# A bank freed inside the second operands of FFN 1, weights split at other places, a product order changed by one swap

## The chip, the cores and the metric

The program runs on one core of a Trainium2 chip. A core has a matrix engine (TensorE, PE in the profile), a vector engine (VectorE, DVE), a scalar engine (ScalarE, ACT), a general engine (GpSimd, POOL) and a queue engine (SyncE, SP) that issues most of the transfers. Each engine takes its instructions in the order of the program; semaphores tie the engines together. The metric is the device time of the program in microseconds, the median of three runs.

## The reference

A two-layer decoder trunk of width 1024 on 1024 tokens, in float32. Layer 0 mixes the tokens with a short gated convolution, layer 1 with dilated attention (16 heads of 64, three branches of window and dilation, a bias by distance); behind each mixer stands a SwiGLU network whose hidden width is 2816.

```
D_FF = ((8 * D_MODEL // 3 + 255) // 256) * 256
BRANCHES = ((128, 1), (512, 4), (2048, 16))

def short_conv_mixer(h, w_in, conv_k, w_out):
    b, c, u = jnp.split(h @ w_in, 3, axis=-1)
    y = lax.conv_general_dilated(
        c * u, conv_k[:, None, :].astype(u.dtype),
        window_strides=(1,), padding=[(CONV_WIDTH - 1, 0)],
        dimension_numbers=("NWC", "WIO", "NWC"),
        feature_group_count=D_MODEL)
    return (b * y) @ w_out

def dilated_attention_mixer(h, w_qkv, w_out, rel_bias):
    ...
    alpha = jax.nn.softmax(jnp.stack(lses, axis=0), axis=0)
    o = jnp.sum(alpha[..., None] * jnp.stack(outs, axis=0), axis=0)
    return o.reshape(bsz, seq, D_MODEL).astype(h.dtype) @ w_out

def swiglu(h, w_gate, w_up, w_down):
    return (jax.nn.silu(h @ w_gate) * (h @ w_up)) @ w_down

    for i in range(DEPTH):
        h = rms_norm(x, mix_norm[i])
        j = i // N_MIXERS
        if i % N_MIXERS == 0:
            x = x + short_conv_mixer(h, conv_w_in[j], conv_kernel[j], conv_w_out[j])
        else:
            x = x + dilated_attention_mixer(h, attn_w_qkv[j], attn_w_out[j], rel_bias)
        h = rms_norm(x, ffn_norm[i])
        x = x + swiglu(h, ffn_w_gate[i], ffn_w_up[i], ffn_w_down[i])
    return rms_norm(x, final_norm)
```

## The kernel before

**Precision.** A float32 product is made of three matmuls. `split` (L139, L140) cuts a tile into a high part, which ACT copies in the type fp32r, and a low part, which DVE gets by subtracting the high part. High times high, high times low and low times high are summed in a PSUM bank (L575, L576, L577). A weight comes from memory as `raw` (L151, issued by SP), some weights are first combined on DVE (`combo`, L191), and then they are split to `w`. `ensure(i)` makes the program split all weights up to number i of one list; `self.at(u, m)` gives the number of the weight of one product.

**Products.** The projections of the convolution (three of them) and of the gate and up parts of a SwiGLU use a scheme with seven products in place of eight (Winograd's form of Strassen's). A unit u is a block of output columns, and m from 1 to 7 is the product. A product (u, m) is 12 matmuls of 128x512: four blocks along the inner dimension, three matmuls each. `unit_order` (L258 to L285) is a list of the pairs, written by hand, and TensorE follows it.

**Banks.** There are eight PSUM banks. A unit has a bank p (products 1, 6, 7, 4, each added to what is in it) and a bank r (products 5 and 3). The first four units of a stage have product 2 in a bank q of its own. After products 1, 6 and 7, ACT copies p to a tile (`save`, L581: tiles u1, u2, u3), and the next product goes into p only behind that copy. `first(u)` adds q to u1 (L585, DVE); with it q is free. In FFN 1 the list begins with products 1 and 2 of units 0 to 3, which take all eight banks, and then has (4, 1).

**Operands.** The other factor of product m is a combination of the four quarters of the layer's input, in tiles `b` (high part by ACT at L567, low part by DVE at L568). `start(n)` is called ahead of the n-th product of the list and puts these preparations between the products, so that what it issues stands ahead of that product's saves in the queues of ACT and DVE. In a SwiGLU, `second_half` (from L1172) is a generator that makes the operands of products 7, 6, 4, 5 and 3 in steps: t3 is multiplied by rstd (L1181), the sums t2 and the differences f − t2, the multiplied h, and h − t2 follow. `mix` does this for the convolution (`start` at L1066 to L1125, with the operand sums at L936 and L937).

**Attention.** Heads are treated in pairs. Scores are at L1487 and L1488, the additions of the bias and the maxima behind them, the maximum over partitions on POOL (L1542), the exponentials at L1550 and L1551 (ACT), and the products with the values at L1561. `values` copies the two halves of its sums by ACT to z (the denominators, L1584) and o (L1585). `finish` takes the logarithm of z (L1616) and exp of its negative (L1618), multiplies o (L1610) and splits it to o_hi and o_lo; L369 to L371 multiply that with the output weights, and L506 adds to x. `first_weights` (L1632 to L1650) splits the first four weights of FFN 1 ahead, its high parts at L1644 and its low parts at L1648. The index `ahead_ao` says up to which output weight is split ahead of the last slot.

The function `after(n)` (L1817) is called behind each output block of FFN 0; it adds the block to the next norm's sums, and makes a step of the bias tables of attention.

Of the kernel before, what the change touches and what calls it, by code (L numbers as in the profile page):

```python
# [95 lines left out]
def trunk(ctx: ExitStack, tc: tile.TileContext, x, gains_in, cwi, ck, cwo, wqkv, wo, relb,  # L96
# [165 lines left out]
    def unit_order(nu, key):  # L262

        conv = key == CONV
        order = [(0, 1), (1, 1), (0, 2), (1, 2), (2, 1), (2, 2), (3, 1)]
        if conv:
            order += [(3, 2), (4, 1), (4, 2)] + [(u, m) for m in (6, 7, 5, 4, 3) for u in (0, 1)]
            order += [(2, 6), (2, 5), (2, 7)]
        else:
            if key:  # L270
                order = [(u, m) for m in (1, 2) for u in range(4)][:-1]
            order += [(3, 2)] + [(4, 1)] * key + [(u, m) for m in (6, 7, 4, 5, 3) for u in (0, 1)] + [(2, 6), (2, 5), (2, 7)]
        order += [(3, 6), (2, 4), (2, 3), (3, 5), (3, 7)] + [(4, 1)] * (key == 0) + [(3, 4), (3, 3)]
        if not conv:
            for u in range(4, SIMPLE):
                order += [(u, 6), (u, 5), (u, 7), (u + 1, 1), (u, 2), (u, 4), (u, 3)]
            for u in range(SIMPLE, nu, 2):
                order += [(u, 6), (u, 5), (u, 7), (u + 1, 1), (u, 3), (u + 1, 6), (u + 1, 5), (u + 1, 7)]
                deep = [(u + 1, DEEPER + i) for i in DEEP_ORDER]
                order += deep[:4] + [(u + 1, 3), deep[4]] + [(u + 2, 1)] * (u + 2 < nu) + deep[5:]  # L280
            return order
        for u in range(4, nu - 1):
            order += [(u, 6), (u, 5), (u, 7), (u + 1, 1), (u + 1, 2), (u, 4), (u, 3)]
        u = nu - 1
        return order + [(u, m) for m in (6, 5, 7, 4, 3)]  # L285

# [616 lines left out]
    class Conv(Strassen):  # L903
# [167 lines left out]
        def mix(self, group1):  # L1071
# [3 lines left out]
            def start(n):  # L1075
# [6 lines left out]
                elif n == 2:  # L1082
                    self.first(0)
                    ensure(self.at(4, 2))
                    next(prep)
                elif n == 3:
                    self.first(1)
                    combos[CONV, 0](6)
                elif n == 4:
# [16 lines left out]
                elif n == 10:  # L1106
                    ensure(self.at(1, 5))
                elif n == 11:
                    next(prep)
                elif n == 12:  # L1110
                    next(prep)
                    ensure(self.at(1, 4))
                elif n == 14:
                    next(prep, None)
                    ensure(self.at(1, 3))
                    X[:] = [None] * KT
                elif n == 18:
                    self.ahead = 3
# [21 lines left out]
    class Swiglu(Strassen):  # L1140
# [38 lines left out]
        def second_half(self):  # L1179
# [6 lines left out]
            for k in range(4):  # L1186
                tt(t3[k], t3[k], rstd, ALU.mult)
                low7.append(self.hi(7, k, t3[k]))
            for k in range(4):
                tt(t2[k], t3[k], f[k], ALU.add)  # L1190
# [42 lines left out]
        def feed_forward(self, stats, last_step, after, final=None):  # L1233
            prep = []

            def start(n):
# [130 lines left out]
    def attention(norm):  # L1367
# [107 lines left out]
        def scores(p, a, st):  # L1475
# [34 lines left out]
            m = page("m")  # L1510
            st["m"] = m
            yield

            for j in range(0, 8, 2):
                b = bank()
                for i in range(2):
# [4 lines left out]
                    else:  # L1521
# [32 lines left out]
        def values(p, a, st):  # L1554
            lf, lh, ld, lp = (st[n] for n in ("lf", "lh", "ld", "lp"))
            acc = [bank(), bank()]
            kd = [[128, 4], [1, 32]]
# [21 lines left out]
            o, z = st["o"], st["z"]  # L1579
            n0 = slice(64 * a, 64 * a + 64)  # L1580
            z0 = slice(64 - 64 * a, 128 - 64 * a)
            for ih in range(2):
                s = slice(ih * HALF, (ih + 1) * HALF)
                nc.scalar.activation(z[n0, s], acc[ih][z0], AF.Copy)  # L1584
                nc.scalar.activation(o[n0, s], acc[ih][n0], AF.Copy)  # L1585
            yield

        def finish(p):
# [25 lines left out]

            next(weights)
            nc.scalar.activation(z, z, AF.Ln)  # L1616
# [192 lines left out]
    with tc.tile_pool(name="first", bufs=1) as scope["pool"]:  # L1809
# [158 lines left out]
```

## Time and profile before

| | |
|---|---|
| time, median of three runs | 2168.83 us (2168.51 to 2171.3) |
| profiled execution | 2170.33 us, its span 2168.5 us |
| mean granted clock of TensorE | 0.994 |
| VectorE, adds at L585 | 153.8 us in 328 instructions |
| transfers | 306.72 MB, mean 141 GB/s |

The row of the engines' busy time, the list of waits and the timelines are in the prediction. A row of a timeline gives the start in us from the beginning of the span, the duration, engine, line, operation, what it writes and reads, the count, and in brackets the idle time of the engine ahead of it with what ended it. A wait is put down to the releaser that came last.

### The profile page before, as it was taken

The page shows a single profiled execution, that of the slowest core. Times are in us where ns is not written, and L with a number is a line of the kernel's source. Part 1 is how long each engine was busy: PE and PEld are TensorE (multiplying, and loading weights), DVE is VectorE, ACT ScalarE, POOL GpSimd, SP SyncE. Part 2 cuts the span into 40 slices and gives each one's busy share as a digit, 9 for nine tenths or more (in the row PEclk, how much of TensorE's full clock was granted, in tenths as well). Part 3 has the DMA queues.
Part 4 walks back from the last instruction along what each step waited for, and adds up shares of the span by engine and source line. Part 5 has one row for each costly group of instructions (what it writes and reads, how often), then busy time and mean ns, then how long its engine had stood idle before and what let it go on. Part 6 is the DMA issues. An engine that isn't in the chain of part 4 may idle for free.

```text
span 2168.5 us, 30735 instructions
## 1 busy us (share of the span) xinstructions
PE 2125.6 (98%) x11086; PEld 1818.7 (84%) x11086; DVE 1728.9 (80%) x3160; ACT 1002.3 (46%) x1797; POOL 222.7 (10%) x316
## 2 busy tenths in 40 slices
PE   9999999999999999999999999999799999999998
PEld 7788887888888888879999998887688888888887
DVE  7898769888888888864777676867788898888886
ACT  7433426444544444334545454536434444534435
POOL 2000001111212000010111111110011211100000
PEclk9999999999999999999999999999899999999999
DMA  7222643335545774341333233544024555586432
GB/s 210 68 93 68 228 141 88 126 122 168 168 156 185 270 284 160 91 149 47 91 83 104 81 105 106 167 135 151 25 93 141 165 173 173 170 315 225 160 93 78
DMA packets 148067, 306.72 MB, mean 141 GB/s; under 512 B 49850, under 2 KB 61130, under 8 KB 147914
## 3 DMA queue, kind: packets, MB, share of 16 engines
q1 hardware_dynamic: 82026, 206.83, 29.9%
q0 software_dynamic: 25872, 79.02, 10.4%
q10 hardware_dynamic: 40016, 18.90, 3.0%
q8 instruction: 88, 1.44, 0.3%
q14 instruction: 65, 0.53, 0.1%
HBM read 209.06 MB, written 88.28 MB: 137 GB/s over the span
## 4 chain that ended last, share of the span: by engine, by line
PE 75%; issue 11%; DVE 6%; DMA 4%; ACT 3%; POOL 1%; SPq 0%; POOLq 0%; ACTq 0%; DVEq 0%
PE bank L575 16%; PE bank L577 16%; PE bank L576 16%; PE bank L369 4%; PE bank L371 4%; PE bank L370 4%; PE bank L1561 4%; PE bank L670 2%; PE bank L673 2%; PE bank L672 2%; PE bank L1488 1%; PE bank L1487 1%; DMA acc<-sq 1%; PE bank L1428 1%; PE bank L1427 1%
## 5 line engine op out<-in xcount | busy, mean ns | idle before, releaser
L575 PE MATMUL bank<-b,w 128*128 128x512 f32 x1816 | 711.4, 392 | 18.9 <-DVE part L585 15.4
L577 PE MATMUL bank<-b,w 128*128 128x512 f32 x1816 | 708.2, 390 | 2.3 <-DVE w L140 2.3
L576 PE MATMUL bank<-b,w 128*128 128x512 f32 x1816 | 709.0, 390 | 0.5 <-DVE b L916 0.5
L575 PEld LDWEIGHTS bank<-b,w 128*128 128x128 f32 x1816 | 341.9, 188 | 93.5 <-DVE part L585 13.5
L577 PEld LDWEIGHTS bank<-b,w 128*128 128x128 f32 x1816 | 341.6, 188 | 74.7 <-DVE w L140 3.8
L576 PEld LDWEIGHTS bank<-b,w 128*128 128x128 f32 x1816 | 341.9, 188 | 71.5 <-DVE b L916 1.8
L139 ACT ACTIVATE w<-combo 128x512 fp32r<-128x512 f32 (+2 forms) x448 | 229.1, 540 | 244.5 <-DVE combo L191 224.4
L140 DVE TENSOR_TENSOR w<-combo,w 128x512 fp32r<-128x512 f32 (+2 forms) x448 | 254.0, 580 | 27.5 <-ACT w L139 27.2
L581 ACT ACTIVATE part<-bank 128x512 f32<-128x512 f32 x168 | 100.1, 596 | 309.4 <-PE bank L577 305.9
L140 DVE TENSOR_TENSOR w<-raw,w 128x512 fp32r<-128x512 f32 (+2 forms) x308 | 169.0, 567 | 26.6 <-ACT w L139 26.4
L585 DVE TENSOR_TENSOR part<-part,bank 128x256 f32<-128x256 f32 (+1 forms) x328 | 153.8, 498 | 38.5 <-ACT part L581 23.8
L139 ACT ACTIVATE w<-raw 128x512 fp32r<-128x512 f32 (+2 forms) x308 | 151.0, 527 | 68.6 <-DMA raw<-in_ffn_w_down 18.0
L831 DVE TENSOR_TENSOR x<-x,bank 128x512 f32<-128x512 f32 x168 | 114.4, 681 | 37.6 <-PE bank L577 33.8
L369 PE MATMUL bank<-w_hi,w 128*128 128x512 f32 (+1 forms) x320 | 120.1, 375 | 0.0
L371 PE MATMUL bank<-w_hi,w 128*128 128x512 f32 (+1 forms) x320 | 118.1, 369 | 0.9 <-DVE w L140 0.9
L370 PE MATMUL bank<-w_lo,w 128*128 128x512 f32 (+1 forms) x320 | 118.0, 369 | 0.0
L506 DVE TENSOR_TENSOR x<-x,bank 128x512 f32<-128x512 f32 (+1 forms) x104 | 65.8, 642 | 60.9 <-PE bank L371 52.2
L369 PE MATMUL bank<-h_hi,w_hi 128*128 128x512 f32 x256 | 104.5, 408 | 0.0
L191 DVE TENSOR_TENSOR combo<-raw 128x512 f32<-128x512 f32 (+1 forms) x160 | 102.9, 643 | 0.0
L371 PE MATMUL bank<-h_hi,w_lo 128*128 128x512 f32 x256 | 100.1, 391 | 0.2 <-DVE w_lo L140 0.2
L370 PE MATMUL bank<-h_lo,w_hi 128*128 128x512 f32 x256 | 100.0, 390 | 0.0
L1542 POOL PARTITION_ALL_REDUCE mb<-m x16 | 53.1, 3317 | 399.2 <-DVE m L1539 216.6
(265 smaller groups left out, 3808.7 us busy)
## 6 DMA issues: line engine op xcount, KB each, us to landing
hin<-part SPq DMA_DIRECT2D x126, 256.0 KB
raw<-in_ffn_w_gate SPq DMA_DIRECT2D x44, 512.0 KB
raw<-in_ffn_w_up SPq DMA_DIRECT2D x44, 512.0 KB
b<-ready SPq DMA_DIRECT2D x42, 512.0 KB
part<-sum POOLq DMA_DIRECT2D x72, 256.0 KB, 3.6
raw<-in_ffn_w_down SPq DMA_DIRECT2D x48, 384.0 KB
x<-spill SPq DMA_DIRECT2D x24, 512.0 KB
raw<-in_attn_w_qkv SPq DMA_DIRECT2D x24, 512.0 KB
```

Of the source, the lines that this page charges most:

```text
L139: nc.scalar.activation(hi, src, AF.Copy)
L140: eng.tensor_tensor(out=lo, in0=src, in1=hi, op=ALU.subtract)
L191: eng.tensor_tensor(out=c, in0=a, in1=b, op=op)
L369: nc.tensor.matmul(b, whi[:, a], ahi[:, s], start=first, stop=False)
L370: nc.tensor.matmul(b, whi[:, a], alo[:, s], start=False, stop=False)
L371: nc.tensor.matmul(b, wlo[:, a], ahi[:, s], start=False, stop=last)
L575: nc.tensor.matmul(b, hi[:, a], bhi, start=start and k == 0, stop=False, skip_group_check=True)
L576: nc.tensor.matmul(b, hi[:, a], blo, start=False, stop=False, skip_group_check=True)
L577: nc.tensor.matmul(b, lo[:, a], bhi, start=False, stop=k == n - 1, skip_group_check=True)
L581: nc.scalar.activation(t, b, AF.Copy)
L585: nc.vector.tensor_tensor(out=t, in0=t, in1=b, op=ALU.add)
L831: nc.vector.tensor_tensor(out=X[n][:, half(h)], in0=X[n][:, half(h)], in1=b, op=ALU.add)
```

## The change

It has five parts, and the arithmetic stays as it was.

- **Unit order.** In the list, (3, 7) stands ahead of (3, 5), and in the last unit of the convolution 7 stands ahead of 5.
- **Convolution start.** `ensure(self.at(4, 2))` goes behind `first(1)`, with `self.at(3, 2)` left where it was; weights (1, 4) and (0, 3) are split ahead of the operand steps of n = 12 and n = 14.
- **SwiGLU start.** In FFN 1, `second_half` stops behind t3, and its next step begins with `first(0)`, now taken at n = 4, with its own step; and at each operand step the weight of the product three places on is split ahead of it, in both networks.
- **Attention.** `values` copies a half of z and o as soon as its four blocks are done, in place of both at the end; the maxima of the second half stand ahead of the loop, those of the first at j = 2 in place of 4. At the end, three output weights in place of seven are split ahead of the last slot, the logarithm's table is loaded and the weights of FFN 1 are stepped there, and the other four slabs follow behind the slot.
- **`after(n)`** splits its weight ahead of `norm.add(n)`.

```diff
@@ unit_order
-        order += [(3, 6), (2, 4), (2, 3), (3, 5), (3, 7)] + [(4, 1)] * (key == 0) + [(3, 4), (3, 3)]
+        order += [(3, 6), (2, 4), (2, 3), (3, 7), (3, 5)] + [(4, 1)] * (key == 0) + [(3, 4), (3, 3)]
...
-        return order + [(u, m) for m in (6, 5, 7, 4, 3)]
+        return order + [(u, m) for m in (6, 7, 5, 4, 3)]
@@ mix, start
                 elif n == 2:
                     self.first(0)
-                    ensure(self.at(4, 2))
+                    ensure(self.at(3, 2))
                     next(prep)
                 elif n == 3:
                     self.first(1)
+                    ensure(self.at(4, 2))
                     combos[CONV, 0](6)
...
                 elif n == 12:
+                    ensure(self.at(1, 4))
                     next(prep)
-                    ensure(self.at(1, 4))
                 elif n == 14:
+                    ensure(self.at(0, 3))
                     next(prep, None)
                     ensure(self.at(1, 3))
@@ second_half
                 tt(t3[k], t3[k], rstd, ALU.mult)
                 low7.append(self.hi(7, k, t3[k]))
+            if self.key:
+                yield
+                self.first(0)
             for k in range(4):
                 tt(t2[k], t3[k], f[k], ALU.add)
@@ feed_forward, start
                 elif n == 4:
                     ensure(self.at(1, 7))
-                elif n in (5, 7, 8, 9, 11):
+                if n in (5, 7, 8, 9, 11) or n == 4 and self.key:
+                    ensure(self.base + n + 3)
                     next(prep[0], None)
@@ scores
             m = page("m")
             st["m"] = m
+            nc.vector.tensor_tensor(out=m[:, HALF:], in0=lf[:, HALF:], in1=lh, op=ALU.max)
             yield
...
-                if j == 0:
-                    nc.vector.tensor_tensor(out=m[:, HALF:], in0=lf[:, HALF:], in1=lh, op=ALU.max)
-                if j == 4:
+                if j == 2:
                     nc.vector.tensor_tensor(out=m[:, :HALF], in0=lf[:, :HALF], in1=ld[:, :HALF], op=ALU.max)
@@ values
                     mm(j // 4, off, b1, j - 1, view(lp, blk(j), b1), last=j % 4 == 3)
+                if j % 4 == 3:
+                    ih, s = j // 4, half(j // 4)
+                    nc.scalar.activation(z[n0, s], acc[ih][z0], AF.Copy)
+                    nc.scalar.activation(o[n0, s], acc[ih][n0], AF.Copy)
                 yield
...
-            for ih in range(2):
-                s = slice(ih * HALF, (ih + 1) * HALF)
-                nc.scalar.activation(z[n0, s], acc[ih][z0], AF.Copy)
-                nc.scalar.activation(o[n0, s], acc[ih][n0], AF.Copy)
-            yield
@@ finish
-            next(weights)
             nc.scalar.activation(z, z, AF.Ln)
@@ attention
-        ahead_ao = [k for k, f in ops].index(("ao", 1, AO_WIDE + 1))
+        ahead_ao = [k for k, f in ops].index(("ao", 1, 2))
...
         ensure(ahead_ao)
+        next(weights)
+        nc.scalar.activation(scratch, eps, AF.Ln)
         slot(H, dense, 20)
         run(dense)
+        ensure(ahead_ao + 4)
@@ after
+            if n in (0, 2):
+                ensure(op_state[1] + 1)
             norm.add(n)
             nc.gpsimd.dma_start(spill[n], X[n])
             if n in (0, 2):
-                ensure(op_state[1] + 1)
                 next(tab, None)
```

What this does to the queues is seen at three places. First VectorE at the start of FFN 1, before. The rows with `x<-x,rstd` are t3 and, further down, h; L568 makes low parts of operands, L140 those of weights, and L585 is the add of `first(0)`.

```order
L140 TENSOR_TENSOR w<-raw,w 128x512 x3
L140 TENSOR_TENSOR w<-combo,w 128x512 x2
L1181 TENSOR_TENSOR x<-x,rstd 128x512 x4
L1181 TENSOR_TENSOR x<-x,hcol 128x512 x2
...
L568 TENSOR_TENSOR b<-x,b 128x512 x6
L140 TENSOR_TENSOR w<-combo,w 128x512 x2
L1181 TENSOR_TENSOR hcol<-hcol,x 128x512 x4
L1181 TENSOR_TENSOR x<-x,rstd 128x512 x4
L568 TENSOR_TENSOR b<-hcol,b 128x512 x4
L1181 TENSOR_TENSOR hcol<-x 128x512 x4
L585 TENSOR_TENSOR part<-part,bank 128x512
```

The same place in the changed kernel, where the lines are two further on:

```order
L140 TENSOR_TENSOR w<-raw,w 128x512 x3
L140 TENSOR_TENSOR w<-combo,w 128x512 x2
L1183 TENSOR_TENSOR x<-x,rstd 128x512 x4
L140 TENSOR_TENSOR w<-combo,w 128x512 x2
L585 TENSOR_TENSOR part<-part,bank 128x512
L1183 TENSOR_TENSOR x<-x,hcol 128x512 x2
...
L568 TENSOR_TENSOR b<-x,b 128x512 x6
L1183 TENSOR_TENSOR hcol<-hcol,x 128x512 x4
L1183 TENSOR_TENSOR x<-x,rstd 128x512 x4
L568 TENSOR_TENSOR b<-hcol,b 128x512 x4
L1183 TENSOR_TENSOR hcol<-x 128x512 x4
```

The add and the pair of weights that stood behind the operands of products 7 and 6 now stand ahead of them. On ScalarE at the same place, in the changed kernel, L567 makes high parts of operands, L581 is a save, and the rows from `x` and `hcol` are the operands 7, 6, 4 and 5 in turn:

```order
L567 ACTIVATE b<-x 128x512 x4
L1258 ACT_TABLE_LOAD
L1258 ACTIVATE scratch<-eps 128x1
L139 ACTIVATE w<-combo 128x512 x2
L567 ACTIVATE b<-x 128x512 x4
L567 ACTIVATE b<-hcol 128x512 x4
L581 ACTIVATE part<-bank 128x512 x2
L567 ACTIVATE b<-hcol 128x512 x4
L581 ACTIVATE part<-bank 128x512
```

Before, the first row had eight copies and the fifth was missing; the saves stand behind the operands 4 and 5 in both. Last, ScalarE at the end of attention in the changed kernel: from the last weights (`raw`, three in place of seven) over the copies of z and o to the operand o_hi of the output product.

```order
L139 ACTIVATE w<-raw 128x384 x3
L1771 ACT_TABLE_LOAD
L1771 ACTIVATE scratch<-eps 128x1
L1588 ACTIVATE z<-bank 64x512
L1589 ACTIVATE o<-bank 64x512
...
L1619 ACTIVATE z<-z 128x1024
L1621 ACT_TABLE_LOAD
L1621 ACTIVATE z<-z 128x512
L139 ACTIVATE o_hi<-o 128x512
...
L139 ACTIVATE w<-raw 128x384 x4
```

Four weights went from ahead of the copies to behind the second o_hi, and a table load from behind the copies to ahead of them.

More of the change, by code (lines that the diff above doesn't have):

```diff
@@ L1555, in values @@
             lf, lh, ld, lp = (st[n] for n in ("lf", "lh", "ld", "lp"))
+            o, z = st["o"], st["z"]
+            n0 = slice(64 * a, 64 * a + 64)
+            z0 = slice(64 - 64 * a, 128 - 64 * a)
             acc = [bank(), bank()]
@@ L1577, in values @@
                     mm(j // 4, off, b1, j - 1, view(lp, blk(j), b1), last=j % 4 == 3)
+                if j % 4 == 3:
+                    ih, s = j // 4, half(j // 4)
+                    nc.scalar.activation(z[n0, s], acc[ih][z0], AF.Copy)
+                    nc.scalar.activation(o[n0, s], acc[ih][n0], AF.Copy)
                 yield
-            o, z = st["o"], st["z"]
-            n0 = slice(64 * a, 64 * a + 64)
-            z0 = slice(64 - 64 * a, 128 - 64 * a)
-            for ih in range(2):
-                s = slice(ih * HALF, (ih + 1) * HALF)
-                nc.scalar.activation(z[n0, s], acc[ih][z0], AF.Copy)
-                nc.scalar.activation(o[n0, s], acc[ih][n0], AF.Copy)
-            yield
         def finish(p):
```

## The prediction

> **What bounds the kernel now.** I read the page first, then the list of what TensorE waited for, then the timelines around the longest of those waits. In the page, the row of TensorE (PE):
>
> ```profile
> PE 2125.6 (98%) x11086; PEld 1818.7 (84%) x11086; DVE 1728.9 (80%) x3160; ACT 1002.3 (46%) x1797; POOL 222.7 (10%) x316
> ```
>
> TensorE bounds the whole span, and the change moves none of its instructions. So the time can change only by the gaps between matmuls. The waits of TensorE, by line, with their total, count and longest:
>
> ```profile
> PE bank L575 <- DVE part L585: 15.4, 2, 13.0
> PE bank L369 <- ACT o_hi L139: 3.3, 1, 3.3
> PE bank L1487 <- ACT o L1585: 2.3, 4, 0.6
> PE bank L577 <- DVE w L140: 2.3, 3, 1.0
> PE bank L1561 <- ACT lf L1551: 2.3, 3, 1.1
> PE bank L575 <- ACT part L581: 2.1, 3, 0.7
> PE bank L575 <- ACT w L139: 0.9, 2, 0.6
> ```
>
> Two rows hold most of it. Their matmuls, with the last product before the long wait, and the granted clock (in a window's row the third number from the end) around the two longest waits:
>
> ```profile
> 1527.36 0.39 PE L575 MATMUL bank<-b,w 128*128 128x512 f32 x1
> 1529.86 0.39 PE L577 MATMUL bank<-b,w 128*128 128x512 f32 x1
> 1543.29 0.79 PE L575 MATMUL bank<-b,w 128*128 128x512 f32 x1 [13.04 <-DVE part L585]
> 1548.57 0.63 PE L575 MATMUL bank<-b,w 128*128 128x512 f32 x1
> ...
> 1471.67 0.80 PE L369 MATMUL bank<-o_hi,w 128*128 128x512 f32 x1 [3.29 <-ACT o_hi L139]
> ...
> 34.62 0.47 PE L575 MATMUL bank<-b,w 128*128 128x512 f32 x1 [2.36 <-DVE part L585]
> ...
> 1470.62:1477.45 6.83, 5.78 (x13) 4.28 (x14) 5.27 (x10) 3.08 (x6) 0.00 (x0) 0.50 0.06 25
> 1535.47:1549.13 13.66, 5.84 (x14) 4.59 (x15) 7.76 (x13) 0.97 (x3) 0.00 (x0) 0.50 0.00 0
> ```
>
> The first two rows are the first and the last matmul of one product: 11 steps in 2.50 us, 0.227 us each, 2.72 us a product. From 1543.29 to 1548.57 twelve steps take 5.28 us: behind a long wait the clock is half (0.50), and the stretch of half speed costs 5.28 − 2.72 = 2.6 us and a little more at its edge, 2.8. After 3.29 us of waiting the 13 matmuls until 1477.45 took 5.78 us instead of 13 × 0.227 = 2.95: 2.8 again. After 2.36 us the next matmul took 0.47 and the pace was full again: no half speed.
>
> **FFN 1 start: bank and operands.** The vector engine (DVE) and ScalarE (ACT) there, before:
>
> ```profile
> 1521.89 2.49 DVE L1181 TENSOR_TENSOR x<-x,rstd 128x512 f32<-128x512 f32 x4
> 1531.72 1.28 DVE L140 TENSOR_TENSOR w<-combo,w 128x512 fp32r<-128x512 f32 x2
> 1532.92 2.49 DVE L1181 TENSOR_TENSOR hcol<-hcol,x 128x512 f32<-128x512 f32 x4
> 1535.33 2.49 DVE L1181 TENSOR_TENSOR x<-x,rstd 128x512 f32<-128x512 f32 x4
> 1537.74 2.49 DVE L568 TENSOR_TENSOR b<-hcol,b 128x512 fp32r<-128x512 f32 x4
> 1540.14 2.49 DVE L1181 TENSOR_TENSOR hcol<-x 128x512 f32<-128x512 f32 x4
> 1542.55 0.68 DVE L585 TENSOR_TENSOR part<-part,bank 128x512 f32<-128x512 f32 x1
> ...
> 1522.61 3.64 ACT L567 ACTIVATE b<-x 128x512 fp32r<-128x512 f32 x6 [2.45 <-DVE x L1181]
> 1528.87 1.28 ACT L1253 ACT_TABLE_LOAD   x1
> 1530.28 1.13 ACT L139 ACTIVATE w<-combo 128x512 fp32r<-128x512 f32 x2
> 1533.72 2.40 ACT L567 ACTIVATE b<-hcol 128x512 fp32r<-128x512 f32 x4 [2.31 <-DVE hcol L1181]
> 1548.81 0.60 ACT L581 ACTIVATE part<-bank 128x512 f32<-128x512 f32 x1 [12.69 <-PE bank L577]
> ```
>
> The add that frees the bank for product (4,1) stands last of some 30 operand instructions. In the new order it follows t3 and one pair of weights. ACT: the four copies of t3 end at 1522.61 + 4 × 0.60 = 1525.0, the table load at 1526.3, the pair of weights at 1527.5; DVE's L140 pair runs from 1527.1 to 1528.3, the add to 1529.0. The product before ends at 1530.08, so the wait of 13.04 us goes, with 1.1 us to spare.
>
> What is late next: DVE has 12 operand instructions of 0.60 behind the add (to 1536.3), then the four rows of 2.41 that stand at 1532.92 to 1540.14, now 3.4 us later. ACT takes its instructions in order. The saves of (4,1) and (0,6) stand behind the four L567 of operand 4, which end at 1539.4; two saves at 0.60 let product (0,7) start at 1540.6 where it could at 1538.24 (1530.08 + 3 × 2.72): **2.4 us**. The save of (1,6) stands behind operand 5, whose last input comes at 1546.1; copy and save bring 1547.3, where (1,7) could start at 1543.3: **4.0 us**. One product later (0,4) starts at 1550.1; now it does so at 1559.8 (1548.57, the slow edge of 0.3, and four products). That is 9.7 us less before any new half speed. A wait of 4.0 us is longer than the 3.29 that brought it, so I charge one stretch, 2.8: **6.9 us** (without it 9.7; with two stretches 4.1).
>
> [...]
>
> **Product order of unit 3 and of the last unit.** Product (3,7) comes ahead of (3,5), and in the last unit of the convolution 7 ahead of 5, so that a product stands between the save of product 5 and product 4 or 3 in its bank:
>
> ```profile
> 95.23 0.50 PE L575 MATMUL bank<-b,w 128*128 128x512 f32 x1 [0.69 <-ACT part L581]
> ```
>
> This is one of the three waits of the row with 2.1 us; with the slow restart (0.50 against 0.39, the next step 0.33) each is 0.85. A save takes 0.60, the product now between takes 2.72. **2.5 us**; nothing if a product's weights came late instead.
>
> **Attention's end.** ACT before, from the last weights to the operand that TensorE waited for:
>
> ```profile
> 1458.55 0.53 ACT L139 ACTIVATE w<-raw 128x384 fp32r<-128x384 f32 x1 [0.46 <-DVE w_lo L140]
> 1463.43 0.59 ACT L1584 ACTIVATE z<-bank 64x512 f32<-64x512 f32 x1
> 1465.87 1.28 ACT L1616 ACT_TABLE_LOAD   x1
> 1467.16 1.06 ACT L1616 ACTIVATE z<-z 128x1024 f32<-128x1024 f32 x1
> 1469.54 0.63 ACT L1618 ACTIVATE z<-z 128x512 f32<-128x512 f32 x1
> 1470.99 0.63 ACT L139 ACTIVATE o_hi<-o 128x512 fp32r<-128x512 f32 x1 [0.82 <-DVE o L1610]
> ```
>
> Four of seven weight slabs leave the queue ahead of 1463.43; the table of Ln is loaded ahead of the copies. The third slab ends at 1459.1, the load at 1460.4, four copies at 0.61 at 1462.9, Ln 1464.0, the load for Exp 1465.3, Exp 1465.9, product and o_hi 1467.4. TensorE's earlier work ends at 1468.2: the wait (3.45 with its restart) and the stretch of half speed (2.8) go. The four slabs now come behind o_hi: the first has its low half at about 1471.7, where the tenth matmul wants it at 1470.7. So 6.25 − 1.05 = **5.2 us**; 2.4 if half speed comes all the same, 6.25 if the slab is in time.
>
> [...]
>
> **Convolution start.** DVE before:
>
> ```profile
> 23.09 1.29 DVE L140 TENSOR_TENSOR w<-raw,w 128x512 fp32r<-128x512 f32 x2 [0.54 <-ACT w L139]
> 26.31 0.69 DVE L140 TENSOR_TENSOR w<-raw,w 128x512 fp32r<-128x512 f32 x1 [1.93 <-ACT w L139]
> 33.80 0.68 DVE L585 TENSOR_TENSOR part<-part,bank 128x512 f32<-128x512 f32 x1
> ```
>
> The weights of (4,1) and (4,2), which waited for a transfer until 26.31, now stand behind the add of 33.80. The seven operand instructions before that add took 4.95 us from 28.85; from 24.3 they bring it to 29.3. But the low weights of (4,1) come behind it, at 30.5, some 0.8 late. Of the 2.52 of this wait 1.75 go. Further on, weights (1,4) and (0,3) are split ahead of operands: four waits (0.9 in the L139 row, 1.77 of the 2.3 in the L140 row) go with their restarts, 3.3; the operand low halves come three DVE instructions later, 1.8 us, of which I charge 1.5. Together **3.5 us**; 0 if DVE's backlog eats it, 5 if the operands are covered.
>
> **Small edits.** Weights ahead of operands at FFN 0 take the third L140 wait, 0.56 and restart: **0.7**. Two waits of weights lose about two thirds, one L140 (0.60) coming earlier in each: **1.2**.
>
> ```profile
> 957.89 0.50 PE L371 MATMUL bank<-w_hi,w 128*128 128x512 f32 x1 [0.85 <-DVE w L140]
> 1444.71 0.50 PE L371 MATMUL bank<-w_hi,w_lo 128*128 128x512 f32 x1 [0.83 <-DVE w_lo L140]
> ```
>
> Attention's copies by half were in this order on ACT already, and the bank that L1487 waits for (0.6 each) is still one of those copied last: these waits stay. The maxima of the softmax come earlier, and with them POOL's reduction, so the three L1561 waits (2.3, 2.8 with restarts) shrink, between 0 and 2.8: I take the middle, **1.4**. SP's queue has the spill loads ahead of three weight loads at attention's end; those weights are split later than before, which covers it.
>
> **Sum.** 6.9 + 2.5 + 5.2 + 3.5 + 0.7 + 1.2 + 1.4 = 21.4 us. The profiled execution took 2170.33 (span 2168.5), which would be 2148.9; the median of the runs, 2168.83, is 1.5 lower, so the forecast is **2147.4**.
>
> **Rivals.** *The saves don't bind* (ACT runs ahead of DVE's operands, or half speed stays away): FFN 1 gains up to 16 (13.2 + 2.8), and with the upper ends of the others the time is about 2138. For it: FFN 0 has the same steps and no such wait. Against: there no table load and no add stand in the chain. Chance 0.13. *Half of it is given back* (new waits for weights at the convolution and attention's end, a second stretch at FFN 1): 4.1 (FFN 1) + 2.4 (attention's end) + 2.5 (order) + 1 (convolution) + 1 (the small ones) = 11, time 2158. For it: each of these places has a margin of 1 us or less. Chance 0.22. *The change doesn't do what it says*: the add stays behind the weights of (1,7) because ACT's table load is late. Then the bank comes a little late, 1 to 3 us, but not 13; it lies in the former. *Slower*: half speed that persists. At FFN 1 two waits follow each other within 8 us; if every window behind them stays at 0.50, each us of it costs half a us, and 21.4 us are lost after 43 us, 13 windows of 3.41. Against: at 1549.13 and 1477.45 the clock came back as soon as one window was full of matmuls. It decides only from 43 us on, then 2172 to 2176. Chance 0.02.
>
> **How the numbers follow.** Forecast 0.60, the first rival 0.13, the second 0.22, no gain at all (2165 to 2173) 0.03, slower 0.02. A measurement of this kernel tells about 0.2%, 4.3 us. Faster 0.95, same 0.03, slower 0.02. The range reaches from 2136 to 2158, and leaves out about 2 in 10.
>
> **What would show it.** Right: L575's wait for L585 falls from 15.4 below 2; in its place waits of L575 for L581 near 2.4 and 4.0 behind the start of FFN 1, with one stretch of half speed; no wait of L369 for o_hi, full clock there; no L581 waits of 0.7. Wrong: saves without a wait (more gain), or DVE's wait for w at the convolution growing (less).

## The result and the profile after

The changed kernel takes 2151.82 us in the median of four runs (2150.50 to 2153.65), the kernel before 2169.06 (2168.51 to 2171.30). The ratio is 0.9919 with a 95% interval of 0.9902 to 0.9936: faster by 17 us (0.8%), where 21.4 were forecast. The profiled execution has a span of 2151.1 us against 2168.5.

The engines' busy time on the page after the change:

```profile
PE 2122.8 (99%) x11086; PEld 1817.6 (84%) x11086; DVE 1728.4 (80%) x3160; ACT 1002.3 (47%) x1798; POOL 221.2 (10%) x316
```

And what TensorE waited for, by line (the lines have moved: L1487 is L1493 now, L1561 is L1569):

```profile
PE bank L575 <- ACT part L581: 6.5, 3, 3.6
PE bank L1493 <- ACT o L1589: 2.3, 4, 0.6
PE bank L575 <- DVE part L585: 1.6, 1, 1.6
PE bank L575 <- ACT w L139: 1.4, 2, 1.2
PE bank L576 <- DVE b L568: 1.2, 1, 1.2
PE bank L371 <- DVE w L140: 1.1, 1, 1.1
PE bank L369 <- ACT o_hi L139: 1.1, 1, 1.1
```

The wait of 13.0 us for the add at L585 is gone, and so are the three for lf. At the top now are waits for saves (L581), as the forecast had it; further down stand one for L585 that it had not, and one for o_hi (1.1 us) that it said would go.

Both programs issue the same 11086 matmuls in the same order but for the two swaps. So the start of the n-th matmul in one profile against its start in the other gives the lead that the changed kernel has at that point, and where it wins or loses. All times are in us from the start of the span; a slow window is a stretch of 3.41 us at half clock (0.50 from 942.91 to 946.32 in the changed kernel).

| matmul | before | after | lead | what lies ahead of it |
|---|---|---|---|---|
| 280 | 72.53 | 68.78 | 3.8 | the convolution's start |
| 400 | 100.80 | 96.06 | 4.7 | the swap in unit 3 |
| 1040 | 246.84 | 243.96 | 2.9 | the convolution's last unit |
| 1640 | 383.74 | 380.89 | 2.9 | the start of FFN 0 |
| 4440 | 949.10 | 948.07 | 1.0 | the bias tables (a slow window) |
| 4560 | 978.04 | 975.33 | 2.7 | the end of FFN 0 |
| 7600 | 1442.82 | 1437.45 | 5.4 | attention |
| 7760 | 1480.55 | 1471.37 | 9.2 | attention's end |
| 8040 | 1560.67 | 1544.43 | 16.2 | the start of FFN 1 |
| 8240 | 1606.99 | 1589.76 | 17.2 | the swap in unit 3 of FFN 1 |
| last | 2161.52 | 2144.57 | 17.0 | |

FFN 1's start, in the timelines of VectorE, ScalarE and TensorE:

```profile
1517.95 1.29 DVE L140 TENSOR_TENSOR w<-combo,w 128x512 fp32r<-128x512 f32 x2 [2.73 <-ACT w L139]
1519.16 0.68 DVE L585 TENSOR_TENSOR part<-part,bank 128x512 f32<-128x512 f32 x1
1527.17 2.49 DVE L1183 TENSOR_TENSOR hcol<-hcol,x 128x512 f32<-128x512 f32 x4
1534.40 2.49 DVE L1183 TENSOR_TENSOR hcol<-x 128x512 f32<-128x512 f32 x4
...
1528.25 2.19 ACT L567 ACTIVATE b<-hcol 128x512 fp32r<-128x512 f32 x4 [3.88 <-DVE hcol L1183]
1530.35 1.06 ACT L581 ACTIVATE part<-bank 128x512 f32<-128x512 f32 x2
1535.17 2.39 ACT L567 ACTIVATE b<-hcol 128x512 fp32r<-128x512 f32 x4 [3.76 <-issue]
1537.46 0.58 ACT L581 ACTIVATE part<-bank 128x512 f32<-128x512 f32 x1
...
1531.46 0.50 PE L575 MATMUL bank<-b,w 128*128 128x512 f32 x1 [2.23 <-ACT part L581]
1538.10 0.80 PE L575 MATMUL bank<-b,w 128*128 128x512 f32 x1 [3.62 <-ACT part L581]
```

Around the second of TensorE's rows, a window (the third number from the end is the granted clock):

```profile
1536.83:1543.66 6.83, 5.56 (x13) 4.40 (x14) 6.09 (x11) 4.98 (x11) 0.00 (x0) 0.50 0.01 2
```

Read from top to bottom: the add comes at 1519.16, and TensorE doesn't stop for the bank. It stops at 1531.46 and 1538.10, each time for a save that ACT could only begin when its four copies of an operand were through. ACT itself was idle for 3.88 and 3.76 us ahead of those copies; it waited for VectorE's differences with the save standing behind. (For the second idle stretch the profile names no releaser; VectorE's four differences begin at 1534.40, 0.8 us ahead of the copies.) Half speed begins inside the second wait, at 1536.83, and lasts two windows.

### The profile page after: what moved, and what is told of

Same layout as the page of the kernel before. It is cut to its first block, busy times and chain, and to the rows that moved or that the text cites. A ratio compares the mean times of both kernels' runs of the same rounds, so it can differ in the third digit from the quotient of the medians.

```text
span 2151.1 us, 30732 instructions
## 1 busy us (share of the span) xinstructions
PE 2122.8 (99%) x11086; PEld 1817.6 (84%) x11086; DVE 1728.4 (80%) x3160; ACT 1002.3 (47%) x1798; POOL 221.2 (10%) x316
## 4 chain that ended last, share of the span: by engine, by line
PE 78%; issue 11%; DVE 4%; DMA 4%; ACT 3%; POOL 0%; SPq 0%; ACTq 0%; POOLq 0%; DVEq 0%
PE bank L575 16%; PE bank L576 16%; PE bank L577 16%; PE bank L369 4%; PE bank L371 4%; PE bank L370 4%; PE bank L1569 4%; PE bank L670 2%; PE bank L673 2%; PE bank L672 2%; PE bank L1494 1%; PE bank L1493 1%; DMA acc<-sq 1%; PE bank L1434 1%; PE bank L1433 1%
## 5 line engine op out<-in xcount | busy, mean ns | idle before, releaser
L140 DVE TENSOR_TENSOR w<-combo,w 128x512 fp32r<-128x512 f32 (+2 forms) x448 | 254.6, 581 | 30.8 <-ACT w L139 30.6
L581 ACT ACTIVATE part<-bank 128x512 f32<-128x512 f32 x168 | 100.0, 596 | 300.9 <-PE bank L577 297.2
L140 DVE TENSOR_TENSOR w<-raw,w 128x512 fp32r<-128x512 f32 (+2 forms) x308 | 169.4, 568 | 22.4 <-ACT w L139 22.1
L585 DVE TENSOR_TENSOR part<-part,bank 128x256 f32<-128x256 f32 (+1 forms) x328 | 154.4, 501 | 38.6 <-ACT part L581 23.1
L369 PE MATMUL bank<-w_hi,w 128*128 128x512 f32 (+1 forms) x320 | 120.2, 376 | 0.0
L369 PE MATMUL bank<-h_hi,w_hi 128*128 128x512 f32 x256 | 104.4, 408 | 0.0
```

Of the source, the lines that this page charges most:

```text
L140: eng.tensor_tensor(out=lo, in0=src, in1=hi, op=ALU.subtract)
L369: nc.tensor.matmul(b, whi[:, a], ahi[:, s], start=first, stop=False)
L581: nc.scalar.activation(t, b, AF.Copy)
L585: nc.vector.tensor_tensor(out=t, in0=t, in1=b, op=ALU.add)
```

## The experiments

Each kernel below is the changed one with the edit shown. Where no interval is given, the time is of one execution; the comparison then goes by the matmuls' starts, place by place.

**The early bank undone.**

```diff
-            if self.key:
-                yield
-                self.first(0)
...
-                if n in (5, 7, 8, 9, 11) or n == 4 and self.key:
+                if n in (5, 7, 8, 9, 11):
```

> The changed kernel with the early add at the start of FFN 1 taken out (no stop behind t3, the steps of the operands at n = 5, 7, 8, 9, 11 as before). Theory (the early bank is worth the wait of 13.0 us and its slow stretch, less the two waits for saves that replaced it): product (4,1) waits 13.0 us for the add at L585 again, the waits of 2.2 and 3.6 us for L581 go, and FFN 1's start costs 7.1 us more than in the changed kernel. Rival (the shift of 9 us ahead of FFN 1 alone gave part of the gain, for instance by another phase of the half-speed windows): under 5 us.

Measured: 2161.40 us. TensorE's wait for the bank in this kernel:

```profile
1536.32 0.80 PE L575 MATMUL bank<-b,w 128*128 128x512 f32 x1 [11.43 <-DVE part L585]
```

It is 11.4 in place of 13.0 since a slow window at 1507.19 had delayed TensorE by 1.6 us ahead of it (it was 2.2 us behind the changed kernel ahead of that window, and stopped 3.8 behind), which the wait took in: VectorE's chain ends when it ends. From a matmul ahead of that window to one behind the waits the kernel loses 6.7 us on the changed one (2.2 behind, then 8.9); from behind the window it would be 5.0, but the 1.6 us of the window are then missing from the wait. Both waits for saves are gone. So the early bank is worth 6.7 us by itself, 7.1 in the first comparison.

**Saves ahead of the copies that held them up.**

```diff
-                if n in (5, 7, 8, 9, 11) or n == 4 and self.key:
+                if n == 8 and self.key:
+                    self.first(1)
+                if n in ((4, 5, 9, 10, 12, 14) if self.key else (5, 7, 8, 9, 11)):
```

> The changed kernel with the operand steps of FFN 1's second operands moved behind the saves that they held up (steps at n = 4, 5, 9, 10, 12, 14 in place of 4, 5, 7, 8, 9, 11, and the second q bank freed at n = 8). Theory (the 2.2 and 3.6 us are ACT's order alone): both waits go, with the half-speed stretch behind them, 8 to 9 us less at FFN 1's start than in the changed kernel. Rival (DVE's operand chain is the bound, the saves only showed it): TensorE waits for b instead at product 4 or 5, and no more than 3 us are gained.

Measured: 2148.69 us. Up to matmul 8040 the kernel wins 8.1 us, as the theory has it: both waits for L581 and the half speed are gone. Then 1.7 and 2.6 us are given back, in new waits of TensorE:

```profile
1535.32 0.50 PE L577 MATMUL bank<-b,w 128*128 128x512 f32 x1 [0.61 <-DVE w L140]
1545.13 0.50 PE L577 MATMUL bank<-b,w 128*128 128x512 f32 x1 [0.67 <-DVE w L140]
1550.03 0.47 PE L575 MATMUL bank<-b,w 128*128 128x512 f32 x1 [2.34 <-DVE part L585]
```

The busy time of the engines over this stretch, in the same kernel:

```profile
1516.00:1551.00 35.00, 31.28 (x133) 24.35 (x132) 33.23 (x55) 19.68 (x35) 1.68 (x3) 1.00 0.11 38
```

The third engine in the row is VectorE: 33.2 busy of 35.0 us. So the waits for saves came from the place of the operand steps, and behind them VectorE's work is the bound of this stretch. (The edit moves VectorE's part of the steps along with ACT's.) Neither expectation held whole: 3.9 us stay.

**The last unit of the convolution in its old order.**

```diff
-        return order + [(u, m) for m in (6, 7, 5, 4, 3)]
+        return order + [(u, m) for m in (6, 5, 7, 4, 3)]
```

> The changed kernel with the last unit of the convolution in its old order (6, 5, 7, 4, 3). Theory (7 straight behind 6 brings the save's wait back, and the add of u3 comes later, so the swap cost time there): the wait of 1.57 us for L585 near 243 us goes, one wait of 0.69 us for L581 stays, 1.7 us less. Rival (the late add is due to other work moved in the convolution): the 1.57 us stay.

Measured: 2149.79 us. In the changed kernel TensorE and VectorE had, in this unit:

```profile
232.91 0.50 PE L575 MATMUL bank<-b,w 128*128 128x512 f32 x1 [0.69 <-ACT part L581]
242.93 0.50 PE L575 MATMUL bank<-b,w 128*128 128x512 f32 x1 [1.57 <-DVE part L585]
...
237.54 1.23 DVE L140 TENSOR_TENSOR w_lo<-hin,w_hi 128x1024 fp32r<-128x1024 f32 x1 [1.70 <-ACT w_hi L139]
242.20 0.68 DVE L585 TENSOR_TENSOR part<-part,bank 128x512 f32<-128x512 f32 x1
```

and with the old order one wait is left:

```profile
238.07 0.50 PE L575 MATMUL bank<-b,w 128*128 128x512 f32 x1 [0.69 <-ACT part L581]
```

From matmul 400 to 1040 the old order wins 1.9 us. The swap moved the save's wait from product 4 to product 7. It also put product 7's save ahead of ACT's next `w_hi`, for which VectorE stood idle 1.70 us; VectorE then ran without a stop from 237.54 and came to the add of u3, which product 3 needs, at 242.20, where product 5 had ended by 238.6. With the old order that idle time isn't there, and the add came at 239.69.

**The third output weight's transfer ahead at attention's end.**

```diff
+        load_raw(raw_state[0])
         acts.update(split_attended(load_attended(range(AO, 7))))
```

> The changed kernel with the transfer of the third output weight at attention's end issued ahead of the loads of the attended pairs on SP's queue. Theory (my forecast missed 2 us there because the third slab landed late: ACT waited 0.83 us for it, and the chain of z behind it): ACT's wait for raw goes, o_hi comes 0.8 us earlier or more, the L369 wait of 1.06 us falls to 0.3 or less; 0.8 to 1.4 us less. Rival (ACT's earlier wait for the attended pairs sets it): o_hi comes at most 0.2 us earlier.

Measured: 2149.76 us. ACT in the changed kernel, then TensorE's wait in it:

```profile
1450.79 1.06 ACT L139 ACTIVATE w_hi<-oin 128x1024 fp32r<-128x1024 f32 x1 [0.20 <-DMA oin<-odram]
1454.50 0.53 ACT L139 ACTIVATE w<-raw 128x384 fp32r<-128x384 f32 x1 [0.83 <-DMA raw<-in_attn_w_out]
1462.76 0.63 ACT L139 ACTIVATE o_hi<-o 128x512 fp32r<-128x512 f32 x1 [0.76 <-DVE o L1614]
...
1463.44 0.50 PE L369 MATMUL bank<-o_hi,w 128*128 128x512 f32 x1 [1.06 <-ACT o_hi L139]
```

and ACT with the transfer ahead:

```profile
1450.61 1.06 ACT L139 ACTIVATE w_hi<-oin 128x1024 fp32r<-128x1024 f32 x1 [0.23 <-DMA oin<-odram]
1451.57 1.33 ACT L139 ACTIVATE w<-raw 128x384 fp32r<-128x384 f32 x3
1460.64 0.63 ACT L139 ACTIVATE o_hi<-o 128x512 fp32r<-128x512 f32 x1 [0.76 <-DVE o L1614]
```

The attended pair is split at the same time (0.2 us apart), the three weights run without a stop, and o_hi comes 2.1 us earlier; TensorE doesn't wait for it. The stretch gains 1.5 us. One thing limits this: where this code is unchanged, the wait of L369 for o_hi was 1.06 us in the changed kernel, 2.17 in the first experiment, 0.17 in the second and 0.15 in the third (in these two the attended pairs had landed apart), and between none and 1.33 in the later ones. So the transfers' times vary from one execution to the next, and the edit's 1.5 us are those of a late execution. What doesn't depend on that is the chain from the split of the second pair to o_hi: 10.0 us in the three kernels with the edit, 10.6 to 12.1 in the nine other profiles that split three weights ahead of the slot.

**Softmax maxima in their old place.**

```diff
-            nc.vector.tensor_tensor(out=m[:, HALF:], in0=lf[:, HALF:], in1=lh, op=ALU.max)
             yield
...
-                if j == 2:
+                if j == 0:
+                    nc.vector.tensor_tensor(out=m[:, HALF:], in0=lf[:, HALF:], in1=lh, op=ALU.max)
+                if j == 4:
```

> The changed kernel with the softmax maxima of the scores where they stood before (second half's at j = 0 in the loop, first half's at j = 4), the copies by half kept. Theory (the earlier maxima start POOL's reduction earlier and took the three L1561 waits away): three waits for lf of 0.6, 1.1 and 0.6 us come back, 2.1 us more over the 16 slots than in the changed kernel. Rival (the copies by half did it): nothing comes back.

Measured: 2155.30 us. In its list of TensorE's waits the row of before is back:

```profile
PE bank L1570 <- ACT lf L1557: 2.3, 3, 1.1
```

The kernel loses 0.5, 0.5 and 1.1 us at the three places, 2.1 in all. The theory held.

**Copies at the end of `values`.**

```diff
-                if j % 4 == 3:
-                    ih, s = j // 4, half(j // 4)
-                    nc.scalar.activation(z[n0, s], acc[ih][z0], AF.Copy)
-                    nc.scalar.activation(o[n0, s], acc[ih][n0], AF.Copy)
                 yield
+            for ih in range(2):
+                s = half(ih)
+                nc.scalar.activation(z[n0, s], acc[ih][z0], AF.Copy)
+                nc.scalar.activation(o[n0, s], acc[ih][n0], AF.Copy)
+            yield
```

> The changed kernel with z and o copied at the end of values, as before, the maxima kept early. Theory (copies by half are worth nothing, their order on ACT was already that): the attention slots last as long as in the changed kernel within 0.3 us, and the four waits of 0.6 us of scores for o stay. Rival (they did it, or half of it): 1 to 2 us more, as waits for lf or for o.

Measured: 2149.83 us. Between matmul 4560 and 7600 its lead on the changed kernel goes from 0.7 to 0.5 us, and the wait of the scores is word for word that of the changed kernel but for the line:

```profile
PE bank L1493 <- ACT o L1590: 2.3, 4, 0.6
```

So the copies by half bring 0.2 us at most in these slots, and the four waits are not theirs. At attention's end this kernel gains 1.7 us more on the changed one, since TensorE doesn't wait for o_hi; its first attended pair was split 3.6 us ahead of the second. Whether the copies' place has a part in that is not shown.

**Without the early load of the logarithm's table.**

```diff
-        nc.scalar.activation(scratch, eps, AF.Ln)
         slot(H, dense, 20)
```

> The changed kernel without the early load of the logarithm's table at attention's end. Theory (the chain to o_hi is ACT's own time there): o_hi comes 1.3 to 1.5 us later behind the copies of z and o, and the wait of L369 grows by as much, 1.3 us in all, or 2.9 if half speed follows. Rival (the load is hidden behind the copies' own wait): no difference over 0.3 us.

Measured: 2153.42 us. ACT in this kernel, from the second attended pair to o_hi:

```profile
1452.04 1.07 ACT L139 ACTIVATE w_hi<-oin 128x1024 fp32r<-128x1024 f32 x1 [0.17 <-DMA oin<-odram]
1455.63 0.52 ACT L139 ACTIVATE w<-raw 128x384 fp32r<-128x384 f32 x1 [0.71 <-DMA raw<-in_attn_w_out]
1463.69 0.63 ACT L139 ACTIVATE o_hi<-o 128x512 fp32r<-128x512 f32 x1 [0.76 <-DVE o L1614]
```

From the third weight to o_hi it takes 8.1 us, with the early load 8.3 (1454.50 to 1462.76). The load is in ACT's queue either way, with nothing to hide behind, so the early place saves nothing. TensorE's wait for o_hi is 1.71 us in place of 1.06 here because the attended pairs landed later (1452.04 against 1450.79, of which 0.3 us is the kernel's lag). The theory fell, and the rival holds by its number, not by its reason.

**FFN 0 without weights ahead of operands.**

```diff
-                    ensure(self.base + n + 3)
+                    if self.key:
+                        ensure(self.base + n + 3)
```

> The changed kernel with the weights ahead of operands in FFN 1 alone, FFN 0 as before. Theory (DVE has no idle time there, so a wait taken away at product 4 comes back at the next product that needs DVE): the wait of 0.6 us at 374 us (its place 371 here) comes back, the one of 0.7 near 379 goes, and the time at 390 us is the same within 0.2 us. Rival (they are two causes): the wait at 374 comes back beside the other, 0.8 us more.

Measured: 2152.26 us. The kernel loses 1.0 us up to matmul 1600 and wins 1.0 back up to 1640. In the changed kernel the wait that took the old one's place, and VectorE ahead of it:

```profile
379.40 0.50 PE L577 MATMUL bank<-b,w 128*128 128x512 f32 x1 [0.69 <-DVE w L140]
...
377.45 0.69 DVE L1233 TENSOR_TENSOR part<-part 128x512 f32<-128x512 f32 x1
378.06 0.68 DVE L191 TENSOR_TENSOR combo<-raw,combo 128x512 f32<-128x512 f32 x1
378.67 0.68 DVE L140 TENSOR_TENSOR w<-combo,w 128x512 fp32r<-128x512 f32 x1
```

None of VectorE's rows has idle time in brackets: it runs through, and a weight taken earlier makes the next one later. The theory held.

**The table matmuls twice.**

```diff
-            nc.tensor.matmul(b[:H, :w], rel, oh[:NBUCKET + 1, :w], start=True, stop=True)
+            for _ in range(2):
+                nc.tensor.matmul(b[:H, :w], rel, oh[:NBUCKET + 1, :w], start=True, stop=True)
```

> The changed kernel with each matmul of the bias tables (33 rows, 16 columns) issued twice, the second writing the same bank again. Theory (a free-running window of 3.41 us in which about 2.4 us or more hold only these small matmuls brings half speed, as in the five of ten profiles whose 2.52 us fell into one window): 5.0 us of them always fill enough of a window, half speed follows at once behind them, 2.5 us for the matmuls and 1.6 for one slow window more. Rival (the coincidence of five profiles was chance, or small matmuls count as work): no slow window there, 2.5 us more alone.

Measured: 2155.92 us. The window that the small matmuls fill, and the next two:

```profile
942.12:945.54 3.42, 3.42 (x13) 1.02 (x11) 2.74 (x4) 3.28 (x3) 0.55 (x1) 1.00 0.37 153
945.54:952.37 6.83, 6.83 (x18) 4.71 (x16) 2.61 (x9) 1.79 (x3) 1.01 (x2) 0.50 0.34 90
```

By its records TensorE is busy throughout, and half speed follows none the less, for two windows. The kernel loses 4.0 us here on the changed one, which has one slow window; 4.1 were expected. What this says of the clock stands below.

**Three edits together**: the saves ahead (with steps at n = 4, 5, 9, 10, 12, 13 and one weight more ahead of the step at n = 9), the last unit's old order, the third weight's transfer ahead.

```diff
+                if n == 8 and self.key:
+                    self.first(1)
+                if n in ((4, 5, 9, 10, 12, 13) if self.key else (5, 7, 8, 9, 11)):
+                    ensure(self.base + n + (4 if n == 9 and self.key else 3))
...
+        return order + [(u, m) for m in (6, 5, 7, 4, 3)]
...
+        load_raw(raw_state[0])
```

> The changed kernel with the operand steps of FFN 1 behind the saves (steps at n = 4, 5, 9, 10, 12, 13, one weight ahead of the step at n = 9, the second q bank freed at n = 8), the last unit of the convolution in its old order, and the third output weight's transfer ahead at attention's end. Theory (the parts add up): 4.5 us at FFN 1, 1.8 in the convolution and 0 to 1.5 at attention's end less than the changed kernel, 2144 to 2146 in the median. Rival (half-speed windows and DVE's backlog take it back): 2148 or more.

Measured: 2147.10 us in the median of four runs (2146.87 to 2148.04), 0.9903 of the kernel before (0.9886 to 0.9919). That is between the two expectations, and 4.7 us under the changed kernel's median. The two were measured beside different runs of the kernel before (2168.50 and 2169.06); by their ratios it is 3.5 us, with intervals that overlap, and by the matmuls' starts in the two profiles 5.2. Of the 9.0 us that it wins at FFN 1's start, 6.8 are given back by matmul 8120, as in the second experiment, and 1.6 of them are a slow window at 1548.77.

**The same with the table matmuls in two halves.**

```diff
+            if c0 == G0:
+                yield
...
-            if n in (0, 2):
+            if n in (0, 2, 3):
                 next(tab, None)
```

> The combined kernel (operand steps of FFN 1 behind the saves, last unit in its old order, third output weight's transfer ahead) with the table matmuls in two halves, behind the third and the fourth output block of FFN 0 in place of all behind the third. Theory (each half is 1.26 us, too little of a window): no half speed there in the profile, and the median falls by the share of executions that had it, about half of 1.6 us: 2146 to 2147, with a spread no larger than 1 us. Rival (the later second half delays the bias tables and the start of attention): 2148 or more, with a wait of the scores' additions for the tables.

Measured: 2148.28 us (2148.12 to 2148.53), 0.9910 of the kernel before (0.9894 to 0.9927), so no gain on the last one. The slow window behind the tables is gone, and the four runs lie within 0.4 us. In its place, behind the second half:

```profile
PE bank L369 <- ACT w L139: 1.3, 1, 1.3
```

It is neither expectation's wait: weights, not tables, come late. From matmul 4400 to 4560 the kernel falls back 1.1 us on the last one, about as much as the medians differ (1.2). The rival's number came out, not its reason, and of the 1.6 us that the theory counted on only 0.5 are there to be won (see below).

## Why the prediction was right, and where its sum was off

The direction, the size class and the main term were right: FFN 1's start was forecast at 6.9 and gave 7.1. That the whole came within 4.4 us of the forecast is in part luck: product order, attention's end, FFN 0 and a slow window that was not counted take 5.6 us off the sum, and the maxima, the convolution and the other terms put 1.3 back. The terms, with what the leads show:

| term | forecast | measured |
|---|---|---|
| FFN 1's start | 6.9 | 7.1 |
| product order | 2.5 | 0.1 |
| attention's end | 5.2 | 3.2 |
| convolution's start | 3.5 | 3.8, of which 0.6 ahead of the edits |
| FFN 0 | 0.7 | 0.0 |
| two waits of weights | 1.2 | 1.9, of which 0.6 by the slow window |
| softmax maxima | 1.4 | 2.1 |
| slow window behind the tables | not in it | -1.6 |

The measured terms make 16.6 of the 17.0 us; small waits that no term named make the rest.

- **FFN 1.** The step held in each part: the bank is free ahead of its product, the waits for saves are 2.23 and 3.62 where 2.4 and 4.0 were forecast, and one stretch of half speed comes with them. The mechanism (ACT in order, a save behind an operand's copies) is shown by the second experiment, in which both waits go when the operand steps stand behind the saves.
- **Product order.** The failed step is "a product stands between the save of product 5 and product 4 or 3 in its bank". Product 5 isn't saved; the wait that goes is product 4's for the save of 7. Unit 3 did what was said, about 1.0 us in each of the two places (0.85 for the wait). In the convolution's last unit 7 now stands straight behind 6, and waits for its save; and the sum u3 + r, which product 3 needs, came 3.6 us behind product 5's end, since VectorE had been held up by ACT's copy behind the save of 7. I had looked at the wait that goes and not at the two neighbours that the swap makes. The third experiment gives 1.9 us back.
- **Attention's end.** The chain of ACT was forecast from the third weight on, and that weight came 1.95 us later than laid out (1454.50, 1460.5 in the clock of before, where it stood at 1458.55). The failed step is "those weights are split later than before, which covers it": that holds for the last four, but the transfer of the third of the first three was behind the loads of the attended pairs on SP's queue (issued at 1451.87, the pairs' loads at 1444.94). Of the 1.95 us, 0.6 are a later split of the pairs, 1.4 lie between it and the third weight; the fourth experiment takes these away. The wait for the fourth weight, 1.05 forecast, was 1.11. The half speed did go.
- **Two waits of weights.** Of the 1.9 us, 0.6 are there only because the slow window ahead gave the weight time. The five profiles of changed kernels that have no such window lose 0.6 us on the changed kernel at the same place (matmul 4474) and 0.4 to 0.5 at 4546, again in waits for weights. So the window's net cost is 0.5 us by matmul 4560, and the edits' part of the two waits 1.3, as forecast.
- **Convolution's start.** The wait for the add at L585 gave 1.77 us, 1.75 forecast. The four waits of weights behind it went, but a wait for an operand's low half (1.21 us at 53.02) and one for a weight (1.20 at 62.44) came, and 1.4 us are left where 1.8 were forecast. The other 0.6 us come at 4.4 us, ahead of the edits, and are this execution's: the later kernels, with the same code there, are 0 to 1.2 us behind the changed one at that point. No experiment took these edits out.
- **Softmax and copies.** Their mechanisms are as forecast: the maxima bring the gain, the copies none. The size was mis-set, the middle of 0 to 2.8; it is 2.1, since all three waits go.
- **FFN 0.** The term failed: the wait was VectorE's backlog showing, and moved on by three products, from matmul 1598 (370.31 in the changed kernel) to 1634 (379.40).
- **The rivals.** "The saves don't bind" was false, "half of it is given back" true of two places only. Half speed that persists was not seen: behind FFN 1's waits it lasted 6.83 us, two windows, and the first of them still held 1.27 us of the wait.

## What to carry to other kernels

Where one wait of TensorE goes, lay out the queues behind it to the next three products; here that gave the two new waits to within 0.4 us. A swap in a hand-written order has to be tried against the new neighbours as well as the old wait. On a stretch where the second engine is busy throughout, a wait taken away came back, at FFN 0 three products later; presumably only less work or an earlier start of that engine shortens the stretch, which no run here tried.

## What the runs showed of the hardware

Half speed came without any idle time in TensorE's records (whose ends are modelled). In the changed kernel's profile the eight small matmuls of the bias tables, and the window behind them:

```profile
940.21 2.59 PE L524 MATMUL bank<-oh,rel 33*16 33x512 f32 x8
942.74 0.67 PE L369 MATMUL bank<-w_hi,w 128*128 128x512 f32 x1
```

```profile
942.91:946.32 3.41, 3.41 (x9) 2.63 (x10) 3.41 (x6) 1.57 (x2) 0.46 (x1) 0.50 0.44 123
```

They use 33 rows and 16 columns of the array, and span 2.52 us from their start to the next matmul's, with no wait among them. In the kernel before, the same eight start at 942.82 and take the same 2.52 us, and the clock stays at 1.00 from there to 1470.62. Issued twice (the experiment on them) they fill 942.12 to 945.54, and the clock is 0.50 from 945.54 to 952.37.

The slow stretches had these lengths: 3.41 us behind the tables and 6.83 at FFN 1 in the changed kernel, 6.83 at attention's end and 13.65 at FFN 1 in the kernel before, 13.65 at FFN 1 in the first experiment, 6.83 behind the tables issued twice. These are one, two and four times 3.41. In the kernel before the two starts (1470.62 and 1535.47) lie 64.85 us apart, 19 times 3.413, and in the changed one (942.91 and 1536.83) 593.92 us, 174 times that. An estimate from these numbers, counted on in steps of 3.413 from the starts: the small matmuls lie within one step in the changed kernel (939.49 to 942.91), and in the kernel before a step ends at 944.97, 2.15 us behind their start. Whether the place in the step makes the difference, or the matmuls' size, or the 0.17 to 0.44 us between their starts, was not separated.

Waits brought half speed in some places and not in others. At attention's end before the change TensorE stopped at 1468.38 for 3.29 us, and the granted clock was 0.50 from 1470.62 on, 2.24 us behind the stop. Without the early table, waits of 1.71 and 0.23 us stood there, and the matmuls from 1465.88 to 1468.87 start 0.43 us apart, where those ahead of the wait start 0.23 apart; in the first experiment 2.17 and 0.23 us did the same. With FFN 0 in its old order 1.33 and 0.23 us did not. Nor did the 2.36 us that end at 34.62 before, and behind the 2.23 that end at 1531.46 in the changed kernel the clock stayed at 1.00 until 1536.83, inside the next wait. So a length of wait from which half speed comes was not shown.

At a second place, ahead of FFN 1's products, TensorE waits 0.9 us and then issues eight matmuls of one column each (L485), 1.8 us together. The clock stays at 1.00 behind them in the kernel before (from 1511.83 to 1535.47) and in the changed one (from 1502.66 to 1536.83); in the first experiment the slow window at 1507.19 is the one behind them.

The slow window behind the tables costs 1.6 us where it stands: the changed kernel loses 1.57 there on the kernel before, which has none. By matmul 4560 only 0.5 of it are left, since TensorE waits for weights there without it; the wait of 11.4 us in the first experiment took the 1.6 us of its window in as well. It can be only a small part of the 3.2 us over which the changed kernel's four runs are spread; the rest is not explained here.
